# An encoder kernel whose attention iterations have two or three stretches of projection steps instead of four, and whose order is written out up to the first FFN matmuls

## Chip, cores and metric

The kernel runs on one core of a Trainium2 chip. The metric is the device time of one execution in microseconds (us). Before the change: 658.37, the median of 3 runs (658.31 to 658.42).

## What is computed

Two layers of an encoder on 256 tokens of width 1024, float32. Each layer has two attention groups side by side, one output projection, and a gated MLP with a convolution over positions:

```python
for l in range(DEPTH):                                  # 2 layers
    h = rmsnorm(x, attn_norm[l])
    c_q, c_kv, k_r, q_d, k_d, v_d = split(h @ w_in[l])
    o_a = mla_mixer(c_q, c_kv, k_r, ...)                # 8 heads, q and k of 96, v of 64
    q_d, k_d = rmsnorm(q_d heads), rmsnorm(k_d heads)   # per head, over 64
    o_b = dilated_attention(q_d, k_d, v_d, rel_bias)    # 8 heads of 64, with a bias table
    x = x + concat(o_a, o_b) @ w_out[l]
    x = x + conv_ffn(rmsnorm(x, ffn_norm[l]), w_up, conv_w, conv_b, w_down)
```

Both attention groups are a softmax over 256 keys. `conv_ffn` is an up projection to 2 x 2816 columns, a width-3 convolution over positions, `silu(gate) * up`, and the down projection.

## The kernel before

**Split matmuls.** Every large product runs as three f32r matmuls: high x high, low x high, high x low (`mm` triples at L488 to L490, L933 to L936, L1081 to L1083). Weights stream from HBM in units of up to 1024 columns. `Weights` splits each unit: `split_hi` copies it on ACT (L175, tile `wh`), `split_lo` subtracts on DVE (L188, tile `wl`) and, at the last unit of a loaded tile, starts the next load. `fill` does one of each where a buffer is free (6 of each kind); `get` forces what is missing.

**The head iterations.** After the MLA projections, `layer` runs nine iterations, 0 to 8, inside `tc.manual_schedule`: PE, DVE and ACT keep the order in which the code issues; outside it a scheduler orders them. Iteration n handles a pair of heads: `scores` (L549, two S banks), `maxima`, `exponents`, `normalise`; for the pair before it `turn_p` (L589: four transposes of P into a bank, then an ACT copy), `values` (L598, bank O) and `keep_o`; for the pair after it `turn_qk` (L526, bank A) and `keep_qk`. Iterations 0 to 3 have MLA pairs, 4 to 7 dilated ones. MLA heads turn queries and keys one head at a time, so twice an iteration; dilated heads turn a pair at once, scores come out with 64 rows. Between these, `gemm` issues steps from a list: the last key and the value projections of the dilated group (`gk`, `gv`, six matmuls a step, one per token block and unit), then output projection steps (`ou`, three matmuls a step). `COUNTS` gives the number of steps in each iteration, which before are dealt evenly over four stretches. Both P transposes of an iteration use bank A, and so do the query/key turns.

**Background work.** `extras` holds the norm of the dilated queries and keys: `d_begin` copies and squares the projection on ACT, `d_end` sums squares over each head on DVE (L643), `d_factor` computes the reciprocal root on POOL (`rsqrt`, three Newton steps, after two small integer operations on DVE, L279 and L281) and scales the two token blocks there (L290, tile `nat`). The dilated pair of iteration 4 is turned in iteration 3, and reads these tiles.

**From the heads to the FFN.** The last output steps, the residual additions into `X` (`out_end`), the transposes of X for the FFN (`xT_part`: four transposes, multiply by the gain, high half on ACT, low half on DVE, squares for the row norm on ACT) and the first half of the first four up units (`up(0)`, `up(1)` with k 0 to 3) stand outside `manual_schedule`. `ffn_scale` makes the row factor `r2b` out of the squares (three POOL operations, `rsqrt` on DVE, a matmul with ones, an ACT copy). `gate(j)` multiplies by it, convolves, applies silu; `down(j)` follows three units later:

```python
            if j == 0:
                ffn_scale()
            gate(j, pu)
```

Of the kernel before, what the change touches and what calls it, by code (L numbers as in the profile page):

```python
# [10 lines left out]
F32 = mybir.dt.float32  # L11
# [8 lines left out]
P = 128  # L20
# [27 lines left out]
START = 5  # L48
COUNTS = [3, 4, 4, 4, 4, 4, 5, 4, 3]
WARM = 8  # L50
FIRST = 5
# [85 lines left out]
class Weights:  # L137
# [94 lines left out]
def encoder(ctx: ExitStack, tc: tile.TileContext, wpk, x, prm, cst, oh, rb, pos, out):  # L232
# [32 lines left out]
    def tbank():  # L265
        return psa.tile([P, 512], F32, name=nm("A"), tag="A", bufs=1)
# [243 lines left out]
    class Heads:  # L510
# [98 lines left out]
    def layer(l, sx, late, bias):  # L609
# [49 lines left out]

        def d_factor(i, dst):  # L660
            rsqrt(fd[:, i, :], dv[i], 16, neg=i == 0, pool=True)
            for t in range(2):
                d_scale(i, dst, t)

        def d_scale(i, dst, t):
            v3 = dst[:, t, :].rearrange("p (h d) -> p h d", h=HEADS)
            ptt(v3, v3, head_scale(v3, fd[:, i, :], t), ALU.mult)

# [245 lines left out]
        run(gk[:START - 3])  # L914
        hm = Heads(l, True, qm, km, vbox[0], pairs, fq)
        hm.turn_qk(0)
        hm.keep_qk(0)
# [8 lines left out]
        def out_mm(k, t, c, final=False):  # L926
            hi, lo = W.get(u_out[k])
            if not accs:
                accs.extend([[acc(), acc()], [acc(), acc()]])
            p = pairs[k]  # L930
# [25 lines left out]
        def d_end(i, t):  # L956
            d_sum(i, t, sq.pop((i, t)))
            if t:
                d_var(i)

        extras = {
            0: [idle, idle, lambda: d_begin(0, qd, 0, a_q[0]), lambda: d_begin(0, qd, 1, a_q[1])],
            1: [lambda: d_end(0, 0), lambda: (d_end(0, 1), d_factor(0, qd)), lambda: d_begin(1, kd, 0, a_k[0]),
                lambda: d_begin(1, kd, 1, a_k[1])],
            2: [lambda: d_end(1, 0), lambda: (d_end(1, 1), d_factor(1, kd))],
        }
# [4 lines left out]
        def iteration(n):  # L971
# [5 lines left out]
            turns = list(nxt[0].turns(nxt[1])) if nxt else []  # L977
            slots = 4 if nxt or cur else 2
            share = [len(todo) // slots + (i < len(todo) % slots) for i in range(slots)]

# [10 lines left out]

            side = list(extras.get(n, []))

            def background():
                if side:
                    side.pop(0)()

            if n == 3:
                v_evac(0)
                v_evac(1)  # L1000
            if cur:
                cur[0].scores(cur[1])
                cur[0].maxima(cur[1])
            if prev:
                prev[0].turn_p(prev[1])
            if cur:
                cur[0].maxima(cur[1] + 1)
                cur[0].exponents(cur[1])
            W.fill()
            gemm()  # L1010
            if prev:
                prev[0].turn_p(prev[1] + 1)
            if cur:
                cur[0].exponents(cur[1] + 1)
            background()
            gemm()
            if prev:
                prev[0].values(prev[1])
                prev[0].keep_o(prev[1])
            background()  # L1020
            turn_next()
            if cur:
                cur[0].normalise(cur[1])
            W.fill()
            background()
            gemm()
            turn_next()
            if cur:
                cur[0].normalise(cur[1] + 1)
            background()  # L1030
            gemm()
            W.fill()
            while side:
                background()
# [5 lines left out]
        run(steps)  # L1040
        run(ou[5][2:3])
        W.fill()

        def out_end(t, c):
            out_mm(7, t, c, final=True)
            xs = X[:, t, 512 * c:512 * c + 512]
            tt(xs, accs[t][c], xs, ALU.add)

        run(ou[5][3:])
        out_end(0, 0)  # L1050
        out_end(1, 0)
        run(ou[6][2:])
        xT_part(sf, gf, 0, 0)
        xT_part(sf, gf, 1, 0)
        out_end(0, 1)
        out_end(1, 1)
        W.done(u_out[7])
        W.fill()

# [75 lines left out]
        first = [[acc(), acc()], [bank(), bank()]]  # L1135
        for j in range(2):
            up(j, first[j], range(4))
            W.fill()
        xT_part(sf, gf, 0, 1, tbank())
        xT_part(sf, gf, 1, 1, obank())  # L1140
        for j in range(NF):
# [9 lines left out]
            if j == 0:  # L1151
                box["a"] = [[acc(), acc()], [acc(), acc()]]
# [103 lines left out]
```

## Time and profile before

| what | value |
|---|---|
| median of 3 runs | 658.37 us |
| the profiled execution's own time | 658.61 us |
| its span, first to last instruction | 656.8 us |
| mean granted TensorE clock | 0.995 |
| PE busy | 637.5 us, 97% |
| DVE, ACT, POOL busy | 493.9 (75%), 398.2 (61%), 67.5 us (10%) |
| layer 0's heads, 61.2 to 140.5 | PE busy 75.90 of 79.30 us |
| layer 1's heads, 380.3 to 459.5 | PE busy 75.87 of 79.20 us |
| dense FFN part of layer 0, 160.5 to 330 | PE busy 169.5 of 169.5, DVE 134.4 |

The page gives one profiled execution. Busy times are sums of instruction durations, merged where they overlap; matmuls are pipelined, so that a stretch in which PE is called busy can still hold matmuls that start later than they could. The timeline view lists instructions with their start, duration and the idle time before them, with what released it. The name before `<-` is the tile written, the names after it the tiles read.

### The profile page before, as it was taken

Reading aid. Unit: us, or ns where it says so; the run is one execution under the profiler, and the core shown is the slowest. Engines: PE = TensorE matmul, PEld = TensorE weight load, DVE = VectorE, ACT = ScalarE, POOL = GpSimd, SP = SyncE. Lnnn points to the kernel's source line nnn. Section 1 sums busy time; section 2 is a strip of 40 time slices with the busy share of each in tenths; the row PEclk is TensorE's granted clock in tenths of the full one; section 3 lists DMA queues with packets and bytes.
Section 4 is the critical chain, followed back from the end, with each engine's and each line's share of the span. In section 5 each row is a group of like instructions: output and inputs, shape, how many; then the busy total and the mean of one; then the engine's idle time right before and its main releaser. Section 6 shows DMA issues by size and latency. Waiting matters only on the chain.

```text
span 656.8 us, 10655 instructions
## 1 busy us (share of the span) xinstructions
PE 637.5 (97%) x4018; PEld 555.9 (85%) x4018; DVE 493.9 (75%) x1006; ACT 398.2 (61%) x721; POOL 67.5 (10%) x177
## 2 busy tenths in 40 slices
PE   8999899989999999999999989999899999999997
PEld 7967676679999999999899876667899999999996
DVE  4796766778987777778699766667699777777773
ACT  5982966756655555555478467766386555555551
POOL 3950170000000000000001105400000000000000
PEclk8999999999999999999999999999899999999999
DMA  8759431152664555554347423313157545555401
GB/s 305 268 192 181 172 128 65 65 193 84 235 202 185 193 193 193 193 178 158 107 138 277 155 80 113 128 65 129 65 172 277 184 172 176 185 189 189 161 1 64
DMA packets 17707, 105.19 MB, mean 160 GB/s; under 512 B 2102, under 2 KB 3799, under 8 KB 6648
## 3 DMA queue, kind: packets, MB, share of 16 engines
q1 hardware_dynamic: 17368, 104.17, 46.1%
q8 instruction: 31, 0.51, 0.3%
q10 hardware_dynamic: 288, 0.34, 0.2%
q14 instruction: 20, 0.16, 0.1%
HBM read 103.20 MB, written 1.31 MB: 159 GB/s over the span
## 4 chain that ended last, share of the span: by engine, by line
PE 85%; DVE 5%; POOL 4%; ACT 3%; issue 1%; DMA 1%; SPq 0%; DVEq 0%; ACTq 0%; POOLq 0%
PE S L1083 12%; PE S L1082 12%; PE S L1081 12%; PE acc L1127 6%; PE acc L1126 6%; PE acc L1125 6%; PE acc L490 4%; PE acc L489 4%; PE acc L488 4%; PE O L598 3%; PE S L549 2%; PE A L589 2%; PE acc L933 2%; PE acc L936 2%; PE acc L935 2%; POOL s L295 2%
## 5 line engine op out<-in xcount | busy, mean ns | idle before, releaser
L175 ACT ACTIVATE wh<-raw 128x1024 fp32r<-128x1024 f32 (+3 forms) x188 | 193.1, 1035 | 108.7 <-PE S L1082 64.9
L188 DVE TENSOR_TENSOR wl<-raw,wh 128x1024 fp32r<-128x1024 f32 (+3 forms) x188 | 223.2, 1190 | 26.9 <-ACT wh L175 26.1
L1082 PE MATMUL S<-xl,wh 128*128 128x256 f32 x640 | 181.3, 284 | 0.0
L1083 PE MATMUL S<-xh,wl 128*128 128x256 f32 x640 | 180.9, 283 | 0.0
L1081 PE MATMUL S<-xh,wh 128*128 128x256 f32 x640 | 180.3, 283 | 0.0
L1082 PEld LDWEIGHTS S<-xl,wh 128*128 128x128 f32 x640 | 122.7, 192 | 1.5
L1081 PEld LDWEIGHTS S<-xh,wh 128*128 128x128 f32 x640 | 122.4, 192 | 1.5
L1083 PEld LDWEIGHTS S<-xh,wl 128*128 128x128 f32 x640 | 122.7, 192 | 0.1
L284 DVE SCALAR_TENSOR_TENSOR t<-t,prm_s,t 128x255 f32<-128x255 f32 x176 | 73.9, 478 | 1.0 <-ACT t L287 0.9
L1127 PE MATMUL acc<-wl,mh 128*128 128x512 f32 x176 | 69.4, 394 | 0.0
L1125 PE MATMUL acc<-wh,mh 128*128 128x512 f32 x176 | 69.3, 394 | 0.0
L1126 PE MATMUL acc<-wh,ml 128*128 128x512 f32 x176 | 69.2, 393 | 0.0
L488 PE MATMUL acc<-wh,xh 128*128 128x512 f32 (+2 forms) x160 | 61.8, 387 | 1.0 <-ACT nat L287 0.8
L490 PE MATMUL acc<-wl,xh 128*128 128x512 f32 (+2 forms) x160 | 58.5, 366 | 0.3 <-DVE wl L188 0.3
L489 PE MATMUL acc<-wh,xl 128*128 128x512 f32 (+2 forms) x160 | 58.4, 365 | 0.2 <-DVE xl L284 0.2
L287 ACT ACTIVATE t<-A 128x512 f32<-128x512 f32 (+2 forms) x56 | 28.1, 501 | 45.4 <-PE A L526 23.3
L287 ACT ACTIVATE t<-t,prm_s 128x256 f32<-128x256 f32 x88 | 47.6, 589 | 4.7 <-DVE t L275 4.7
L287 ACT ACTIVATE mh<-t 128x256 fp32r<-128x256 f32 x44 | 18.2, 414 | 47.8 <-DVE t L275 47.8
L275 DVE TENSOR_TENSOR t<-S,r2b 128x512 f32<-128x512 f32 (+1 forms) x42 | 27.9, 665 | 24.0 <-PE S L1083 24.0
L1127 PEld LDWEIGHTS acc<-wl,mh 128*128 128x128 f32 x176 | 33.1, 188 | 7.5
L1125 PEld LDWEIGHTS acc<-wh,mh 128*128 128x128 f32 x176 | 33.4, 190 | 5.9
L1126 PEld LDWEIGHTS acc<-wh,ml 128*128 128x128 f32 x176 | 33.1, 188 | 6.1
(168 smaller groups left out, 974.4 us busy)
## 6 DMA issues: line engine op xcount, KB each, us to landing
raw<-in_wpk_dram SPq DMA_DIRECT2D x86, 1024.0 KB, 4.8
raw<-in_wpk_dram SPq DMA_DIRECT2D x3, 896.0 KB, 4.5
raw<-in_wpk_dram SPq DMA_DIRECT2D x3, 768.0 KB, 4.5
raw<-in_wpk_dram SPq DMA_DIRECT2D x2, 816.0 KB, 5.3
Bn<-scr SPq DMA_DIRECT2D x8, 192.0 KB, 11.2
raw<-in_wpk_dram SPq DMA_DIRECT2D x2, 720.0 KB, 5.8
X<-in_x_dram SPq DMA_DIRECT2D x3, 256.0 KB, 5.1
raw<-in_wpk_dram SPq DMA_DIRECT2D x2, 384.0 KB, 5.5
```

Of the source, the lines that this page charges most:

```text
L175: self.nc.scalar.activation(hi[:, :n], self.raw[t][:, o:o + n], AF.Copy, scale=1.0 if g is None else g)
L188: self.nc.vector.tensor_tensor(out=lo[:, :n], in0=raw, in1=hi, op=ALU.subtract)
L287: nc.scalar.activation(o, a, f, **kw)
L488: mm(o, lhs.hi[:, k, sl], rh, start=k == 0, stop=False)
L489: mm(o, lhs.lo[:, k, sl], rh, start=False, stop=False)
L490: mm(o, lhs.hi[:, k, sl], rl, start=False, stop=k == ktot - 1)
L1081: mm(o, hi[:, kp], sf.hi[:, k, :], start=k == 0, stop=False)
L1082: mm(o, hi[:, kp], sf.lo[:, k, :], start=False, stop=False)
L1083: mm(o, lo[:, kp], sf.hi[:, k, :], start=False, stop=k == 7)
L1125: mm(o, m.hi[:, 0, sl], hi[:, cs], start=j == 0, stop=False)
L1126: mm(o, m.lo[:, 0, sl], hi[:, cs], start=False, stop=False)
L1127: mm(o, m.hi[:, 0, sl], lo[:, cs], start=False, stop=j == NF - 1)
```

## The change

It changes the order of work at the heads and after them; the arithmetic stays.

- In an iteration both P transposes follow the scores directly, the second one of a pair in bank O instead of A. The steps come in two or three stretches (`SHARES`): one, one, one in iteration 0; two, one, one where two query/key turns follow; two and two (or three) where one does.
- `turn_next` comes behind the first stretch; `exponents` of the second head and `normalise` of the first behind it; `values` after that. `fill` is taken apart into `fill_hi` and `fill_lo`, which stand at places of their own.
- The exp table is loaded early by an activation of a constant (`act(small(2)[:, :1], ones[:, :1], AF.Exp)`).
- Sums of squares of the dilated heads go to the start of iterations 1 and 2. The scaling of the dilated keys goes from POOL to DVE, at the start of iteration 3; that of the queries stays on POOL.
- `v_evac` goes behind the first exponents of iteration 3, and the output accumulators are dealt out so that the first two steps use the older pair.
- The order is fixed from iteration 8 through the last output steps and the first halves of `up(0)` and `up(1)`. The squares come behind all four transposes. `ffn_scale` and `gate(0)` move from j = 0 to j = 1.

The diff, cut to its core (`ptt` is a POOL operation, `tt` a DVE one):

```diff
+SHARES = {2: (1, 1, 1), 3: (2, 1, 1), 4: (2, 2, 0), 5: (2, 3, 0)}
...
+    def fill_hi(self):
+        if self.n_hi < min(len(self.units), self.n_done + W_BUFS - W_SLACK):
+            self.split_hi()
+
+    def fill_lo(self):
+        if self.n_lo < self.n_hi:
+            self.split_lo()
...
-            pt = tbank()
+            pt = (obank if i % 2 else tbank)()
...
         extras = {
...
+            0: ([], [], [lambda: d_begin(0, qd, 0, a_q[0]), lambda: d_begin(0, qd, 1, a_q[1])]),
+            1: ([lambda: d_end(0, 0), lambda: d_end(0, 1)], [lambda: d_factor(0, qd)],
+                [lambda: d_begin(1, kd, 0, a_k[0]), lambda: d_begin(1, kd, 1, a_k[1])]),
+            2: ([lambda: d_end(1, 0), lambda: d_end(1, 1)], [lambda: d_factor(1, kd, ())], []),
+            3: ([lambda: d_scale(1, kd, 0, tt), lambda: d_scale(1, kd, 1, tt)], [], []),
...
+            kind = 2 if not prev else 3 if len(turns) == 2 else len(todo)
+            share = list(SHARES[kind]) if kind in SHARES and len(todo) == sum(SHARES[kind]) else [2, len(todo) - 2, 0]
...
+            early, middle, late_ = extras.get(n, ([], [], []))
+            if cur:
+                cur[0].scores(cur[1])
+                cur[0].maxima(cur[1])
+                cur[0].maxima(cur[1] + 1)
+            if prev:
+                prev[0].turn_p(prev[1])
+                prev[0].turn_p(prev[1] + 1)
+            run(early)
+            if not early:
+                W.fill_lo()
+            if cur:
+                cur[0].exponents(cur[1])
             if n == 3:
                 v_evac(0)
                 v_evac(1)
...
             gemm()
+            turn_next()
             if cur:
                 cur[0].exponents(cur[1] + 1)
...
+                cur[0].normalise(cur[1])
+            if early:
+                W.fill_lo()
             if prev:
                 prev[0].values(prev[1])
                 prev[0].keep_o(prev[1])
...
+            run(middle)
+            W.fill_hi()
             gemm()
             turn_next()
             if cur:
                 cur[0].normalise(cur[1] + 1)
...
+            run(late_)
+            W.fill_lo()
+            W.fill_hi()
             gemm()
...
+            out_end(0, 0)
+            out_end(1, 0)
+            run(ou[6][2:3])
+            pv0 = gained(0, 0, xT_turn(0, 0))
+            run(ou[6][3:])
+            pv1 = gained(1, 0, xT_turn(1, 0))
+            W.fill_hi()
+            low(0, 0, pv0)
+            low(1, 0, pv1)
+            W.fill_lo()
+            out_end(0, 1)
+            out_end(1, 1)
...
+            up(0, first[0], range(4))
+            W.fill_hi()
+            W.fill_lo()
+            pv2 = gained(0, 1, xT_turn(0, 1, tbank()))
+            up(1, first[1], range(4))
+            pv3 = gained(1, 1, xT_turn(1, 1, obank()))
+            low(0, 1, pv2)
+            low(1, 1, pv3)
+            xT_square(sf, 0, 1)
+            xT_square(sf, 1, 1)
...
             if j == 0:
+                continue
+            if j == 1:
                 ffn_scale()
+                gate(0, first[0])
             gate(j, pu)
```

`gained` is the gain multiplication on DVE and the copy of the high half on ACT, `low` the subtraction of the low half on DVE; together they are what `xT_keep` did.

What stands where, before and after. First PE in iteration 4 of layer 0, from the first P transposes on (A and O are the banks, `acc` the output accumulators, `nat_171` and `nat_172` the dilated queries and keys, `nat_676` the MLA values). Before:

```order
L589 MATMUL A_1389<-cst_s,t_291_1300 128x128 x4
L933 MATMUL acc_1321<-wh_1105,mh_1200 128x512
L935 MATMUL acc_1321<-wh_1105,ml_1201 128x512
L936 MATMUL acc_1321<-wl_1144,mh_1200 128x512
L589 MATMUL A_1406<-cst_s,t_297_1313 128x128 x4
L933 MATMUL acc_1323<-wh_1105,mh_1200 128x512
L935 MATMUL acc_1323<-wh_1105,ml_1201 128x512
L936 MATMUL acc_1323<-wl_1144,mh_1200 128x512
L598 MATMUL O_1418<-t_321_1394,nat_676 64x256
L598 MATMUL O_1418<-t_326_1411,nat_676 64x256
```

and in the change (its line numbers are higher by 9 to 11):

```order
L598 MATMUL A_1390<-cst_s,t_292_1288 128x128 x4
L598 MATMUL O_1397<-cst_s,t_296_1294 128x128 x4
L944 MATMUL acc_1320<-wh_1251,mh_1214 128x512
L946 MATMUL acc_1320<-wh_1251,ml_1215 128x512
L947 MATMUL acc_1320<-wl_1272,mh_1214 128x512
L944 MATMUL acc_1321<-wh_1251,mh_1214 128x512
L946 MATMUL acc_1321<-wh_1251,ml_1215 128x512
L947 MATMUL acc_1321<-wl_1272,mh_1214 128x512
L535 MATMUL A_1416<-cst_s,nat_171 128x128 x2
L535 MATMUL A_1416<-cst_s,nat_172 128x128 x2
L607 MATMUL O_1431<-t_325_1395,nat_676 64x256
L607 MATMUL O_1431<-t_327_1402,nat_676 64x256
```

The second P transposes stand behind the first, in bank O; two output steps follow in one stretch, then the turn of the next pair, and only then the values.

Second, DVE from the last split but one of iteration 2 into iteration 3 (`wl` a weight split, `ml` the low half of an output pair, `nat_172` the dilated keys). Before:

```order
L188 TENSOR_TENSOR wl_1259<-raw_825,wh_1142 128x1024
L279 TENSOR_SCALAR t_286_1274<-A_1269,gqk 96x256
L580 RECIPROCAL s_1278<-s_1167 128x2
L279 TENSOR_SCALAR t_254_1165<-t_254_1165,s_1278 128x256 x2
L188 TENSOR_TENSOR wl_1290<-raw_923,wh_1257 128x1024
L558 TENSOR_REDUCE s_1303<-S_1294 128x2
L284 SCALAR_TENSOR_TENSOR s_1301<-s_1303,fq_189 128x2
L558 TENSOR_REDUCE s_1316<-S_1295 128x2
L284 SCALAR_TENSOR_TENSOR s_1314<-s_1316,fq_189 128x2
L275 TENSOR_TENSOR ml_1346<-O_1340,mh_1345 128x256
L279 TENSOR_SCALAR t_311_1354<-A_1349,gqk 128x256
```

and in the change:

```order
L284 TENSOR_TENSOR ml_1215<-O_1209,mh_1214 128x256
L288 TENSOR_SCALAR s_1218<-s_1172 128x16
L290 TENSOR_SCALAR s_1219<-s_1218 128x16
L288 TENSOR_SCALAR t_287_1264<-A_1259,gqk 96x256
L589 RECIPROCAL s_1268<-s_1152 128x2
L288 TENSOR_SCALAR t_253_1150<-t_253_1150,s_1268 128x256 x2
L189 TENSOR_TENSOR wl_1272<-raw_825,wh_1251 128x1024
L567 TENSOR_REDUCE s_1291<-S_1282 128x2
L293 SCALAR_TENSOR_TENSOR s_1289<-s_1291,fq_189 128x2
L567 TENSOR_REDUCE s_1297<-S_1283 128x2
L293 SCALAR_TENSOR_TENSOR s_1295<-s_1297,fq_189 128x2
L284 TENSOR_TENSOR nat_172<-nat_172,fd_174 128x512 x2
```

The two integer operations that start the keys' reciprocal root (`s_1218`, `s_1219`) now stand behind `ml` and the sums, which were done earlier; the scaling of the keys, two POOL rows before, is a DVE row behind the maxima of iteration 3.

Third, ACT in layer 0's FFN start, up to the row factor (`xh` the high half of the transposed X, `X` rows are the squares, `wh` weight splits). Before:

```order
L287 ACTIVATE t_412_1839,s_896<-X 128x512
L287 ACTIVATE xh_894<-t_411_1835 128x4x128
L287 ACTIVATE t_415_1850,s_896<-X 128x512
L287 ACTIVATE xh_894<-t_414_1846 128x4x128
L175 ACTIVATE wh_1922<-raw_1530 128x1024
L175 ACTIVATE wh_1972<-raw_1678 128x1024
L287 ACTIVATE r2b_1767<-O_1904 128x256
```

and in the change:

```order
L296 ACTIVATE xh_896<-t_412_1819 128x4x128
L296 ACTIVATE xh_896<-t_414_1851 128x4x128
L296 ACTIVATE t_415_1856,s_898<-X 128x512
L296 ACTIVATE t_416_1858,s_898<-X 128x512
L176 ACTIVATE wh_1951<-raw_1488 128x1024
L176 ACTIVATE wh_1962<-raw_1645 128x1024
L176 ACTIVATE wh_1968<-raw_1645 128x1024
L176 ACTIVATE wh_2053<-raw_1726 128x1024
L296 ACTIVATE r2b_1783<-O_1937 128x256
```

The squares of the second half come behind its high halves, and four splits instead of two stand between them and `r2b`.

## Rows read from the trace of the kernel before

**Rows 1.** The page, part 1: busy time, share of the span and instructions of each engine.
```profile
PE 637.5 (97%) x4018; PEld 555.9 (85%) x4018; DVE 493.9 (75%) x1006; ACT 398.2 (61%) x721; POOL 67.5 (10%) x177
```

**Rows 2.** Windows: length; PE, PEld, DVE, ACT, POOL busy us (instructions); PEclk, DMA share, GB/s.
```profile
61.20:140.50 79.30, 75.90 (x403) 53.56 (x401) 54.75 (x142) 55.81 (x129) 16.20 (x39) 1.00 0.38 124
...
140.50:160.50 20.00, 17.93 (x145) 17.51 (x145) 15.13 (x36) 11.24 (x19) 0.81 (x3) 1.00 0.29 106
459.50:479.50 20.00, 17.93 (x132) 17.44 (x132) 13.56 (x32) 9.69 (x18) 0.81 (x3) 0.91 0.26 91
```

**Rows 3.** Who PE waited for: us in total, times, longest us.
```profile
PE A L526 <- DVE t L279: 4.9, 6, 1.0
```

**Rows 4.** PE timeline, iterations 0 to 3: start us, us, instructions, [idle before, releaser].
```profile
61.22 1.89 PE L549 MATMUL S<-t,t 96*128 96x256 f32 x8
...
68.65 0.42 PE L526 MATMUL A<-cst_s,qm 128*96 128x128 f32 x2 [0.98 <-DVE t L279]
...
81.93 1.89 PE L549 MATMUL S<-t,t 96*128 96x256 f32 x8
83.66 0.60 PE L589 MATMUL A<-cst_s,t 128*128 128x128 f32 x4
...
87.41 1.08 PE L598 MATMUL O<-t,nat 128*64 128x256 f32 x8
```

**Rows 5.** PE timeline, a switch from f32 transposes to f32r matmuls.
```profile
71.86 0.60 PE L589 MATMUL A<-cst_s,t 128*128 128x128 f32 x4
72.22 0.48 PE L488 MATMUL acc<-wh,xh 128*128 128x512 f32 x1
72.53 0.39 PE L489 MATMUL acc<-wh,xl 128*128 128x512 f32 x1
72.76 0.40 PE L490 MATMUL acc<-wl,xh 128*128 128x512 f32 x1
```

**Rows 6.** PE timeline, iterations 3 to 8.
```profile
97.43 1.55 PE L598 MATMUL O<-t,nat 128*64 128x256 f32 x8
...
101.26 1.13 PE L549 MATMUL S<-t,t 64*128 64x256 f32 x8
102.32 0.66 PE L589 MATMUL A<-cst_s,t 128*128 128x128 f32 x4
...
130.23 0.60 PE L589 MATMUL A<-cst_s,t 128*128 128x128 f32 x4
```

**Rows 7.** POOL timeline, rsqrt of the dilated keys.
```profile
90.86 0.21 POOL L290 TENSOR_TENSOR s<-s 128x16 f32<-128x16 f32 x1 [0.50 <-DVE s L281]
...
91.78 1.29 POOL L295 TENSOR_SCALAR s<-s 128x16 f32<-128x16 f32 x1
...
97.19 0.22 POOL L290 TENSOR_TENSOR fd<-s,s 128x16 f32<-128x16 f32 x1
```

**Rows 8.** DVE timeline, same stretch, a split of weights.
```profile
91.79 1.22 DVE L188 TENSOR_TENSOR wl<-raw,wh 128x1024 fp32r<-128x1024 f32 x1
```

**Rows 9.** DVE groups by form, 40 to 60 us: count, busy us, mean ns, idle before.
```profile
L275 DVE TENSOR_TENSOR km<-km,fk 128x512 f32<-128x512 f32 x2 | 1.4, 688 | 0.0
```

**Rows 10.** ACT timeline, before the first key evacuation of layer 0.
```profile
40.61 0.47 ACT L287 ACTIVATE km<-acc,rkv 128x256 f32<-128x256 f32 x1 [1.11 <-DVE rkv L284]
```

**Rows 11.** PE timeline, from the last output step to the FFN, layer 0.
```profile
140.20 0.39 PE L936 MATMUL acc<-wl,mh 128*128 128x512 f32 x1
...
143.91 0.36 PE L1082 MATMUL acc<-xl,wh 128*128 128x256 f32 x1
```

**Rows 12.** ACT timeline, the FFN's row factors.
```profile
155.49 0.36 ACT L287 ACTIVATE r2b<-O 128x256 f32<-128x256 f32 x1
```

**Rows 13.** DVE timeline, low half of the first gate's product.
```profile
164.55 0.42 DVE L275 TENSOR_TENSOR ml<-t,mh 128x256 fp32r<-128x256 f32 x1
```

**Rows 14.** PE timeline, first down matmul.
```profile
167.46 0.39 PE L1125 MATMUL acc<-wh,mh 128*128 128x512 f32 x1
```

**Rows 15.** Window of one microsecond in layer 1's FFN start, with the granted clock.
```profile
463.00:464.00 1.00, 1.00 (x7) 0.50 0.76 320
```

More of the change, by code (lines that the diff above doesn't have):

```diff
@@ L658, in d_var, with d_factor, d_scale @@
                     pts(vv, ssd[:, i, t, :], 1.0 / HD, ALU.mult, sx.e1[:, t:t + 1], ALU.add)
-        def d_factor(i, dst):
+        def d_factor(i, dst, toks=range(2)):
             rsqrt(fd[:, i, :], dv[i], 16, neg=i == 0, pool=True)
-            for t in range(2):
-                d_scale(i, dst, t)
-        def d_scale(i, dst, t):
+            for t in toks:
+                d_scale(i, dst, t, ptt)
+        def d_scale(i, dst, t, mul):
             v3 = dst[:, t, :].rearrange("p (h d) -> p h d", h=HEADS)
-            ptt(v3, v3, head_scale(v3, fd[:, i, :], t), ALU.mult)
+            mul(v3, v3, head_scale(v3, fd[:, i, :], t), ALU.mult)
         a_q, a_k, a_v = Accs(), Accs(), Accs()
@@ L915, in layer @@
         hm = Heads(l, True, qm, km, vbox[0], pairs, fq)
+        act(small(2)[:, :1], ones[:, :1], AF.Exp)
         hm.turn_qk(0)
@@ L928, in out_mm @@
             if not accs:
-                accs.extend([[acc(), acc()], [acc(), acc()]])
+                a = [acc() for _ in range(4)]
+                accs.extend([a[0::2], a[1::2]])
             p = pairs[k]
@@ L961, in layer @@
         extras = {
[L962 to L965, printed above, removed]
+            0: ([], [], [lambda: d_begin(0, qd, 0, a_q[0]), lambda: d_begin(0, qd, 1, a_q[1])]),
[3 more added lines that the diff above has]
+            3: ([lambda: d_scale(1, kd, 0, tt), lambda: d_scale(1, kd, 1, tt)], [], []),
         }
@@ L977, in iteration @@
             turns = list(nxt[0].turns(nxt[1])) if nxt else []
-            slots = 4 if nxt or cur else 2
-            share = [len(todo) // slots + (i < len(todo) % slots) for i in range(slots)]
+            kind = 2 if not prev else 3 if len(turns) == 2 else len(todo)
+            share = list(SHARES[kind]) if kind in SHARES and len(todo) == sum(SHARES[kind]) else [2, len(todo) - 2, 0]
             def gemm():
@@ L990, in turn_next @@
                     nxt[0].keep_qk(i)
[L992 to L996, printed above, removed]
+            early, middle, late_ = extras.get(n, ([], [], []))
[11 more added lines that the diff above has]
+                cur[0].exponents(cur[1])
             if n == 3:
@@ L1019, in iteration @@
                 prev[0].keep_o(prev[1])
[L1020 to L1025, printed above, removed]
+            run(middle)
+            W.fill_hi()
             gemm()
@@ L1029, in iteration @@
                 cur[0].normalise(cur[1] + 1)
-            background()
+            run(late_)
+            W.fill_lo()
+            W.fill_hi()
             gemm()
-            W.fill()
-            while side:
-                background()
             assert not todo
@@ L1039, in layer, with out_end, gained, low @@
                 iteration(n)
[L1040 to L1058, printed above, removed]
+            run(steps)
+            run(ou[5][2:])
+            W.fill_hi()
+            W.fill_lo()
+            def out_end(t, c):
+                out_mm(7, t, c, final=True)
+                xs = X[:, t, 512 * c:512 * c + 512]
+                tt(xs, accs[t][c], xs, ALU.add)
+            def gained(t, c, pt):
+                tv = wide()
+                pv = tv.rearrange("p (k t) -> p k t", k=4)
+                tt(pv, pt.rearrange("p (k t) -> p k t", k=4),
+                   gf[:, 4 * c:4 * c + 4].unsqueeze(2).to_broadcast([P, 4, P]), ALU.mult)
+                act(sf.hi[:, 4 * c:4 * c + 4, t * P:t * P + P], pv, AF.Copy)
+                return pv
+            def low(t, c, pv):
+                sl = slice(t * P, t * P + P)
+                tt(sf.lo[:, 4 * c:4 * c + 4, sl], pv, sf.hi.bitcast(F32)[:, 4 * c:4 * c + 4, sl], ALU.subtract)
+            out_end(0, 0)
[10 more added lines that the diff above has]
+            out_end(1, 1)
+            W.done(u_out[7])
+            xT_square(sf, 0, 0)
+            W.fill_hi()
+            W.fill_lo()
+            xT_square(sf, 1, 0)
         r2b = work.tile([P, SEQ], F32, name=nm("r2b"), tag="r2b", bufs=1)
@@ L1135, in layer @@
         first = [[acc(), acc()], [bank(), bank()]]
[L1136 to L1140, printed above, removed]
+        with tc.manual_schedule(engines={mybir.EngineType.PE, mybir.EngineType.DVE, mybir.EngineType.Activation}):
+            up(0, first[0], range(4))
+            W.fill_hi()
+            W.fill_lo()
+            pv2 = gained(0, 1, xT_turn(0, 1, tbank()))
[5 more added lines that the diff above has]
+            xT_square(sf, 1, 1)
         for j in range(NF):
@@ L1148, in layer @@
             if j == 0:
+                continue
+            if j == 1:
                 ffn_scale()
+                gate(0, first[0])
             gate(j, pu)
-            if j == 0:
+            if j == 1:
                 box["a"] = [[acc(), acc()], [acc(), acc()]]
```

13 lines of the change are left out of this document (removed).

## Prediction

> **What bounds the kernel now.** I read the page's busy shares first: PE is busy 637.5 of 656.8 us, 97% [rows 1], so everything this change can win lies in some 19 us of visible PE idle time, plus idle time that hides inside matmul durations. The windows come next. In layer 0's head iterations PE is busy 75.90 of 79.30 us while DVE (54.75) and ACT (55.81) are each under three quarters full [rows 2]: no other engine is the bound there, PE loses time to the order of small dependent steps. The FFN start shows 17.93 of 20.00 in both layers, and in layer 1 also a mean clock of 0.91 [rows 2]. The list of waits names the largest one: PE's query/key transposes waited six times, 4.9 us in all, for DVE [rows 3]. Layer 1's iterations repeat layer 0's, so I work out one layer and double it.
>
> **Prices, from the timeline.** I count PE work from start to next start, because durations overlap. MLA scores take 1.73 us (81.93 to 83.66) and values 1.08 [rows 4]; four transposes 0.36, a 512-column matmul 0.23 (72.53 to 72.76) and the first one after transposes 0.31, so a change of kind costs 0.08; I charge that in both directions [rows 5]. A projection step of six matmuls is then 1.38, an output step of three 0.69. Dilated scores take 1.06 (101.26 to 102.32) [rows 6].
>
> **Iterations 0 to 3, one layer.** They run from 61.22 to 101.26, 40.04 us [rows 4, 6]. Their work: 4 scores 6.92, 6 P transposes 2.16, 3 values 3.24, 11 projection steps 15.18, 4 output steps 2.76, 7 query/key turns 2.52, 22 changes of kind 1.76; together 34.54. So 5.5 us are lost, with examples in the rows: a turn that idled 0.98 [rows 4], values that took 1.55 instead of 1.08 because the second copy of P had just been asked for [rows 6]. The change removes the causes: a turn is now followed by a projection step or by values before the next turn needs bank A, and the second P lies in bank O directly behind the first, with two steps behind both to hide two copies. I do not credit all 5.5.
>
> A wait stays, and grows. The dilated keys may be turned in iteration 3 only when their rsqrt on POOL and their scaling are done. Before, that rsqrt runs from 90.86 to 97.41, 6.55 us [rows 7]. Two of its operations (the row at 91.78 is one) take 1.29 instead of 0.21 us; that one starts within 0.01 us of a weight split of 1.22 us on DVE [rows 7, 8]. The order of the change puts one split into the chain, so I take 6.55 - 1.08 = 5.47. It began 2.37 us after the values of iteration 2 ended (88.49); in the change the key squares are summed earlier (a gain) and a split lies ahead of the low half of the output (a loss of up to 1.22), so I keep about 2.5. Iteration 2 now lasts 1.73 + 0.72 + 5.52 + 1.08 + 0.72 + 8 x 0.08 = 10.4 us, its values end at 6.8, the chain runs from 9.3 to 14.8, that is to 4.4 in iteration 3. Then DVE, which waits there with all behind it, scales twice at 0.69 (the nearest row is the same operation on the MLA keys, [rows 9]): 5.8. PE comes to that turn at 4.0 (scores, both P, two output steps). It waits 1.8 us; bounds are 0 (chain early) and 4 (a second split in it, and everything a microsecond late). I keep back 0.5 more for waits too small to place. Gain: 5.5 - 1.8 - 0.5 = 3.2.
>
> [...]
>
> **Iterations 4 to 7.** From 101.26 to 130.23 are 28.97 us, of which 0.46 belong to two hoisted matmuls [rows 6]. Work: scores 4.24, P 2.88, values 4.32, 17 output steps 11.73, 3 turns 1.08, 16 changes 1.28: 25.53. Lost are 3.0, nearly all as values waiting for the second P copy. Two output steps of 0.69 now stand behind both transposes, against two copies on ACT, so I credit 2.5; 0.5 again for small waits, the first P of iteration 4 after DVE's late start among them. Gain: 2.5.
>
> Edits I cost at nothing: the early table load, since ACT waits for DVE there anyway (1.11 us idle before the next key evacuation, and a split that stood ahead of it is moved behind [rows 10]), though in layer 0 it may push the keys by a few tenths; the permuted accumulators and later v evacuation, which keep the first two output steps off the value accumulators; the weight loads on SP, each issued behind a tile's last split and so moved with it, since the DMA engines are busy 0.38 of this stretch and four loaded tiles wait [rows 2]; the two POOL scales that go to DVE, counted above.
>
> **FFN start.** The last output step starts at 140.20 and lasts 0.23; PE is dense again at 143.91 [rows 11]. In these 3.48 us it does four matmuls of 256 columns (half of 0.23 each) and eight transposes, 1.2 in all, so 2.3 are lost. In the change the first half's transposes stand two to six matmuls earlier, so the high half is there when up(0) starts; the low half of token block 1 comes after it on DVE, 0.6 us late. Against that, the squares and so the row factor now come last: the ACT order puts four weight splits ahead of r2b, each of which needs a buffer that PE frees only as it finishes the first four up units. I expect r2b some 3.6 us later against PE than at 155.49, where it stood 11.6 us ahead of the first down matmul at 167.46 [rows 12, 14]. From its end to the end of the low half of gate 0's product were 9.1 us (155.85 to 164.97, [rows 12, 13]), so that margin is just used up; I charge 0.6 for the mm of ones and the first down. Lost in the change 1.2, gain 1.1 per layer; bounds -2 and +1.9.
>
> **Clock.** In layer 1 the time lost here is followed by a stretch at half clock, 0.50 in the window at 463 [rows 15]; a mean of 0.91 over 20 us costs 1.8 us, and layer 0, with the same PE busy time of 17.93, shows 1.00 [rows 2]. With the loss cut to parts of 0.6 us I expect it to stay away: 1.6; bounds 0 and 1.8.
>
> **Sum.** 2 x (3.2 + 2.5) + 2 x 1.1 + 1.6 = 15.2. The profiled execution took 658.61 us (span 656.8 and 1.8 around it): 643.4. The median of the runs, 658.37, is 0.24 lower: 643.2.
>
> **Rivals.**
> - *The POOL chain does not bind*, and the half microseconds kept back are not lost: 2 x (1.8 + 1.0) = 5.6 less, 637.6. For it: DVE and ACT are far from full. Against it: even before, the rsqrt ended only at 97.41 with two POOL scales to come, as iteration 3 reached its values (97.43, [rows 6, 7]). 0.12.
> - *The new 1.8 us wait drops the clock*, as one of the two FFN starts did before [rows 2, 15]. One or two falls of 1.8 us: 645 to 646.8. For it: layer 1. Against: the wait in iteration 3 is shorter and has dense matmuls on both sides. 0.17. [...]
> - *The gates come too late*: if each of the four splits ahead of r2b, and DVE's four behind them, ends later than I schedule, PE waits at the first down and at the score banks for up to 3 us a layer: 649. 0.10.
> - *Gains lost again inside the FFN*, because DVE starts its dense part behind and never catches up: 657 to 659. 0.03.
> - *Slower*: the key chain. If DVE, which now runs more two-operand work in iteration 2, held each of the other 15 POOL operations of the chain for a split's 1.08 us, the turn of iteration 3 would wait 16 us longer in each layer: 676. It decides against the change from seven held operations on (7 x 1.08 x 2 = 15.1). Against: only one split stands there. 0.03.
>
> **How the numbers follow.** The forecast, with 0.55, is 643.2, its own range 641 to 647. The range to 8 in 10 takes in the clock case, the late gates and the better part of the first rival: 639 to 650. A measurement of this kernel tells 0.2%, 1.3 us, from no change. Faster by more: forecast and the first three rivals, 0.94; within: 0.03; slower: 0.03.
>
> **What would show it.** Values in iterations 4 to 7 at 1.08, not 1.55; no PE wait for DVE at the query/key transposes of iterations 0 to 2; one PE wait of 1 to 3 us in iteration 3 of each layer, for DVE's scaled keys behind POOL; iterations 0 to 8 some 5.7 us shorter per layer; the FFN start's 2.3 us down to 1.2, layer 1's at clock 1.00; r2b about 3 to 4 us later against the first up matmul, with a PE wait under 1 us. It is wrong if the head iterations shorten by less than 4 us a layer, or if the FFN start loses as much as before.

## The result and the profile after

The changed kernel took 642.16 us (median; 642.15 to 643.89) against 658.39 us of the kernel before on the same chip: ratio 0.9756, 95% interval 0.9736 to 0.9775. The profiled execution took 642.16 us, its span 640.4 us, where before they were 658.61 and 656.8. The forecast was 643.2 us, range 639 to 650: 16.2 us came off where 15.2 were expected. The one execution of 643.89 us has a mean clock of 1.000 on record, so a fall of the clock is not what made it longer; what did stays open.

The page, part 1, of the changed kernel, beside [rows 1]:

```profile
PE 627.8 (98%) x4018; PEld 554.6 (87%) x4018; DVE 497.4 (78%) x1010; ACT 395.8 (62%) x723; POOL 58.9 (9%) x173
```

PE has the same 4018 instructions and is busy 9.7 us less: part of the lost time had stood inside long matmul rows, such as values of 1.55 us in [rows 6], and some of it in the stretch of layer 1 at half clock, 0.50 [rows 15]. Windows of the changed kernel, with the columns of [rows 2]: layer 0 from the first scores to the last output step, then 20 us of the FFN start in layer 0 and in layer 1.

```profile
60.80:133.91 73.11, 71.77 (x403) 53.91 (x401) 55.48 (x144) 50.77 (x124) 12.01 (x37) 1.00 0.41 135
133.91:153.91 20.00, 19.58 (x156) 18.88 (x156) 16.79 (x34) 13.87 (x24) 0.58 (x3) 1.00 0.40 137
445.55:465.55 20.00, 19.58 (x156) 18.89 (x156) 16.79 (x34) 13.95 (x24) 0.58 (x3) 1.00 0.37 139
```

The same 403 PE instructions need 73.11 us instead of 79.30. At the FFN start PE is busy 19.58 of 20 us instead of 17.93, and layer 1's clock there is 1.00 instead of 0.91. Who PE waited for, with the columns of [rows 3] (line 535 is line 526 of the kernel before, the query/key turns):

```profile
PE A L535 <- DVE nat L284: 2.7, 4, 1.1
```

The six waits of [rows 3] are gone. What is left at the turns of the iterations is four waits for `nat`, the dilated keys that DVE scales: the wait that the prediction kept. They are two in each layer. Here is its place, PE's timeline from the turn of iteration 3 into iteration 5 (iteration 4 starts at 96.98):

```profile
92.07 0.38 PE L535 MATMUL A<-cst_s,nat 128*128 128x128 f32 x2
93.52 0.33 PE L535 MATMUL A<-cst_s,nat 128*128 128x128 f32 x1 [1.07 <-DVE nat L284]
94.12 0.33 PE L535 MATMUL A<-cst_s,nat 128*128 128x128 f32 x1 [0.27 <-DVE nat L284]
94.38 1.08 PE L607 MATMUL O<-t,nat 128*64 128x256 f32 x8
...
96.98 1.14 PE L558 MATMUL S<-t,t 64*128 64x256 f32 x8
...
104.58 0.66 PE L598 MATMUL A<-cst_s,t 128*128 128x128 f32 x4
105.07 0.60 PE L598 MATMUL O<-cst_s,t 128*128 128x128 f32 x4
...
106.91 0.60 PE L535 MATMUL A<-cst_s,nat 128*128 128x128 f32 x4
107.44 1.08 PE L607 MATMUL O<-t,natb 128*64 128x256 f32 x8
```

From 92.07 to the values at 94.38 are 2.31 us; the turn of iteration 5 needs 0.53 us (106.91 to 107.44), so 1.78 us are lost. The two transposes of P now stand 0.49 us apart (104.58 and 105.07), the second in bank O, and the values of iteration 5 take 1.08 us. Behind the wait stands POOL's chain, with the weight split on DVE that begins inside it:

```profile
87.28 0.21 POOL L299 TENSOR_TENSOR s<-s 128x16 f32<-128x16 f32 x1 [1.78 <-DVE s L290]
...
88.48 1.27 POOL L299 TENSOR_TENSOR s<-s,s 128x16 f32<-128x16 f32 x1
...
92.51 0.22 POOL L299 TENSOR_TENSOR fd<-s,s 128x16 f32<-128x16 f32 x1
```

```profile
88.46 1.21 DVE L189 TENSOR_TENSOR wl<-raw,wh 128x1024 fp32r<-128x1024 f32 x1
...
92.77 1.29 DVE L284 TENSOR_TENSOR nat<-nat,fd 128x512 f32<-128x512 f32 x2 [1.51 <-POOL fd L299]
```

The chain takes 5.45 us (87.28 to 92.73) and has one long row, 1.27 us. At the FFN start PE waited 2.05 us for the high half of the transposed X in the kernel before:

```profile
142.65 0.51 PE L1081 MATMUL acc<-xh,wh 128*128 128x256 f32 x2 [2.05 <-ACT xh L287]
```

In the changed kernel its timeline shows two small losses, one either side of the first up matmul (lines 1106 and 1107), and none at the matmul of ones (149.18) or the first down matmul (159.56):

```profile
133.68 0.40 PE L947 MATMUL acc<-wl,mh 128*128 128x512 f32 x1
134.13 0.39 PE L1106 MATMUL acc<-xh,wh 128*128 128x256 f32 x1
134.86 0.38 PE L1107 MATMUL acc<-xl,wh 128*128 128x256 f32 x1 [0.34 <-DVE xl L284]
...
149.18 0.59 PE L1093 MATMUL O<-t,ones 128*128 128x256 f32 x2
...
159.56 0.39 PE L1150 MATMUL acc<-wh,mh 128*128 128x512 f32 x1
```

Where the 16.4 us of span came from: iterations 0 to 3 went from 40.04 to 36.16 us (60.82 to 96.98), 3.88 a layer; iterations 4 to 7 from 28.51 (28.97 less the 0.46 of two hoisted matmuls) to 26.31, 2.20 a layer; together 12.2 (layer 0 doubled). From the end of the last output step to the first down matmul, layer 0 went from 27.03 to 25.65 us (1.38) and layer 1 from 28.59 to 25.64 (2.95). That is 16.5. The head iterations also begin 0.40 us earlier ([rows 4]: 61.22; now 60.82), and from the last matmul (652.48 before, 635.59 after) to the end of the span it takes 0.5 us longer; I put neither down to the change. Between the first down matmul and the next layer's first scores nothing moved: 212.83 us before, 212.85 after.

### The profile page after: what moved, and what is told of

Read it like the earlier page. It is cut to its first block, busy times and chain, and to the rows that moved or that the text cites. A ratio compares the mean times of both kernels' runs of the same rounds, so it can differ in the third digit from the quotient of the medians.

```text
span 640.4 us, 10656 instructions
## 1 busy us (share of the span) xinstructions
PE 627.8 (98%) x4018; PEld 554.6 (87%) x4018; DVE 497.4 (78%) x1010; ACT 395.8 (62%) x723; POOL 58.9 (9%) x173
## 4 chain that ended last, share of the span: by engine, by line
PE 89%; DVE 5%; POOL 3%; issue 1%; ACT 1%; DMA 1%; SPq 0%; DVEq 0%
PE S L1108 12%; PE S L1107 12%; PE S L1106 12%; PE acc L1152 6%; PE acc L1151 6%; PE acc L1150 6%; PE acc L499 4%; PE acc L497 4%; PE acc L498 4%; PE S L558 3%; PE acc L944 2%; PE O L607 2%; PE acc L947 2%; PE acc L946 2%; PE A L535 1%; POOL s L304 1%
## 5 line engine op out<-in xcount | busy, mean ns | idle before, releaser
L296 ACT ACTIVATE t<-A 96x256 f32<-96x256 f32 (+2 forms) x40 | 18.8, 469 | 43.8 <-PE A L535 26.6
```

What stands on the lines that cost most here:

```text
L296: nc.scalar.activation(o, a, f, **kw)
```

## The experiments

Where a sentence compares with "the change", the 642.16 us above are meant; the kernel before took 658.62, 659.34 and 658.39 us beside the three groups of runs, each on a chip of its own, so a difference of less than 1 us from the change is not told by the medians; where one matters, it is read from the profiles. A ratio is always to the kernel before.

### Is it the order or the bank?

```diff
-            pt = (obank if i % 2 else tbank)()
+            pt = tbank()
```

> The change with the second P back in bank A, all else as it is. Theory (order and bank O belong together): with both P transposes back to back, the second must wait in every iteration until ACT has copied the first out of bank A (a copy of 0.60 us and the way there and back, some 0.9 us; 16 iterations of two layers), so about 14 us slower than the change: 652 to 658 us, and a PE wait for ACT at the P transposes in each iteration. Rival (the order alone brings the gain, the bank is a detail): 642 to 644 us.

Measured: 655.06 us, ratio 0.9946 (0.9934 to 0.9959), 12.9 us slower than the change. The theory holds: sixteen waits, one in each iteration that turns P. PE's waits and the first place in the timeline:

```profile
PE A L598 <- ACT t L296: 11.1, 16, 0.8
```

```profile
69.56 0.60 PE L598 MATMUL A<-cst_s,t 128*128 128x128 f32 x4
70.91 0.66 PE L598 MATMUL A<-cst_s,t 128*128 128x128 f32 x4 [0.76 <-ACT t L296]
```

The other half alone, in the kernel before:

```diff
-            pt = tbank()
+            pt = (obank if i % 2 else tbank)()
```

> The kernel before with one edit: the second P goes to bank O, its place and order stay. Theory (what PE waited for at the values is the second copy of P, asked for only one step earlier, and not the bank): within 1 us of before, 657.5 to 658.5 us, values in iterations 4 to 7 still 1.5 us and more. Rival (bank A was the bottleneck): most of the 12 us of the head iterations come back, 646 to 650 us.

Measured: 657.53 us, ratio 0.9983 (0.9972 to 0.9994), 1.1 us faster than before. From the first scores to those of iteration 7 are 61.82 us (60.80 to 122.62), before 61.78: nothing. Against the expectation, the values do not take 1.5 us and more: the long row has turned into a wait that the timeline can show, and values of 1.08:

```profile
103.09 0.60 PE L589 MATMUL O<-cst_s,t 128*128 128x128 f32 x4
...
105.10 1.08 PE L598 MATMUL O<-t,nat 128*64 128x256 f32 x8 [0.71 <-ACT t L287]
```

From the first scores to the end of the last output step layer 0 takes 79.21 us in the kernel before, 78.76 with the bank alone, 79.44 with the change less the bank, 73.09 with the change. So the bank alone brings 0.45 us a layer, all behind the first scores of iteration 7, the order alone nothing, and the gain belongs to the pair. Which part of the order removed the six waits of [rows 3] was not tested apart: with the bank alone they are all there, with the order alone they are gone and the waits for P stand in their place.

### How many steps must stand behind the transposes?

```diff
-SHARES = {2: (1, 1, 1), 3: (2, 1, 1), 4: (2, 2, 0), 5: (2, 3, 0)}
+SHARES = {2: (1, 1, 1), 3: (2, 1, 1), 4: (0, 4, 0), 5: (0, 5, 0)}
```

> The change with no output step between the P transposes and the next turn or the values in iterations 3 to 7 (shares 0, 4, 0 for 2, 2, 0): the two steps stand behind the values. Theory (two copies of P on ACT take 1.10 us and must be covered by steps behind both transposes): in iteration 4 the copies end 1.79 us after the first P transposes begin, and without steps PE reaches the values about 0.5 us too early, in iteration 7, which has no turn, about 0.9 us: 0.5 x 3 + 0.9 = 2.4 us per layer, 646 to 647.5 us, PE waiting for ACT at the values. Rival (the turn and the bank are cover enough, or the steps moved behind the values hide another wait): 641.5 to 643 us.

> The change with one output step there in place of two (shares 1, 3, 0). Theory (the copies end 1.79 us after the first P transposes begin; in the change the values of iteration 4 start 1.07 us after that, and one step less takes 0.77 of it): nothing but in iteration 7, which has no turn, 0.2 us per layer: 642 to 642.8 us. Rival (what counts is the number of steps, since ACT's copies are held up by other work when they come): 643.5 to 645 us.

(One step: shares 1, 3, 0 and 1, 4, 0.) Measured: no step 652.49 us, ratio 0.9904 (0.9885 to 0.9922); one step 646.95 us, ratio 0.9816 (0.9799 to 0.9833). Both are outside either range. Without steps, iterations 4 to 6 are 0.45, 0.44 and 0.46 us longer and iteration 7 waits 0.74 us at its values, in size what the theory has. The place in iterations 4 to 6 is another: PE waits at the turn, which needs bank A free of the first P, and not at the values:

```profile
102.47 0.66 PE L535 MATMUL A<-cst_s,nat 128*128 128x128 f32 x4 [0.25 <-ACT t L296]
```

With one step, iterations 4 to 6 last 6.53, 6.52 and 7.23 us, what they last in the change (6.53, 6.55, 7.23). What I had overlooked is that the shares serve iteration 3 too, where the step covers POOL's chain; without steps iteration 3 lasts 11.86 us. With one step, iteration 3 of layer 0 lasts 11.07 us instead of 8.91: first a longer wait, then values of nearly double length. Timeline, then two windows:

```profile
94.64 0.33 PE L535 MATMUL A<-cst_s,nat 128*128 128x128 f32 x1 [1.75 <-DVE nat L284]
...
95.65 1.98 PE L607 MATMUL O<-t,nat 128*64 128x256 f32 x8
```

```profile
96.00:98.00 2.00, 2.00 (x9) 0.92 (x6) 1.79 (x5) 1.56 (x7) 0.00 (x0) 0.50 0.04 8
...
410.00:412.00 2.00, 2.00 (x9) 0.97 (x6) 1.90 (x5) 1.56 (x7) 0.00 (x0) 0.50 0.00 0
```

0.67 us are the missing step, 1.5 us (2.16 less 0.67) the clock, which fell to 0.50 in both layers. To separate the two, one step in iterations 4 to 7 only:

```diff
+            SH = {**SHARES, **({4: (1, 3, 0), 5: (1, 4, 0)} if 4 <= n <= 7 else {})}
-            share = list(SHARES[kind])
+            share = list(SH[kind])
```

> The change with one output step between the P transposes and the turn in iterations 4 to 7 only; iteration 3 keeps its two. Theory (in the run with one step everywhere, iterations 4 to 6 began 6.53, 6.52 and 7.23 us after one another as in the change; its loss is iteration 3's, 0.67 us more wait for the keys and then half clock): 641.9 to 642.8 us, and no stretch at half clock in either layer. Rival (the second step is needed in iterations 4 to 7 too): 643.5 to 645 us.

Measured: 642.56 us, ratio 0.9760 (0.9745 to 0.9775); iterations 3 to 6 of layer 0 last 8.91, 6.53, 6.53 and 7.23 us, clock 1.00. From the first scores to the end of the last output step are 73.24 us, in the change 73.09. So one step is cover enough for two copies of P, to within 0.15 us a layer; the second step earns its place in iteration 3.

### The wait for the keys, longer and shorter

```diff
-            3: ([lambda: d_scale(1, kd, 0, tt), lambda: d_scale(1, kd, 1, tt)], [], []),
+            3: ([lambda: d_scale(1, kd, 0, ptt), lambda: d_scale(1, kd, 1, ptt)], [], []),
```

> The change with the two scalings of the dilated keys in iteration 3 back on POOL (1.03 us each by the row of the queries, against 0.65 on DVE). The wait before the second half of the key turn grows by 0.8 us, to about 2.6 us in all. Theory (a wait of 2 us and more there is followed by half clock, as in both layers of the run with one step everywhere, and that costs 1.5 us each): 2 x (0.8 + 1.5) = 4.6 us slower than the change, 645.5 to 647.5 us, with windows at 0.50 behind iteration 3's turn in most cases. Rival (the fall does not hang on the length of the wait): 643.4 to 644.4 us, clock 1.00 there.

Measured: 646.37 us, ratio 0.9814 (0.9801 to 0.9827). Iteration 3 of layer 0 lasts 11.19 us, 2.28 more than in the change. Timeline and windows:

```profile
93.97 0.33 PE L535 MATMUL A<-cst_s,nat 128*128 128x128 f32 x1 [1.47 <-POOL nat L299]
94.97 0.47 PE L535 MATMUL A<-cst_s,nat 128*128 128x128 f32 x1 [0.67 <-POOL nat L299]
```

```profile
96.00:98.00 2.00, 2.00 (x10) 0.96 (x7) 1.96 (x5) 1.56 (x6) 0.00 (x0) 0.50 0.00 0
...
410.00:412.00 2.00, 2.00 (x10) 0.96 (x7) 1.97 (x5) 1.56 (x6) 0.00 (x0) 0.50 0.00 0
```

The two waits are 0.80 us longer together (2.14 for 1.34), and the other 1.48 us of the 2.28 are the lower clock. Moving the two scalings from POOL to DVE, which I had counted as part of the chain, is thus worth 4.2 us, most of it (twice 1.48) kept clock. Now the wait made shorter:

```diff
-            1: (..., [lambda: d_factor(0, qd)],
+            1: (..., [lambda: d_factor(0, qd, ())],
...
-            2: ([lambda: d_end(1, 0), lambda: d_end(1, 1)], [lambda: d_factor(1, kd, ())], []),
+            2: ([lambda: d_end(1, 0), lambda: d_end(1, 1), lambda: d_scale(0, qd, 0, tt),
+                 lambda: d_scale(0, qd, 1, tt), lambda: d_factor(1, kd, ())], [], []),
```

> The change with the rsqrt of the dilated keys started right behind their square sums in iteration 2 (before: behind the values and a weight split), and the scaling of the dilated queries on DVE in iteration 2, where DVE idles 2.03 us, so that POOL is free for the chain. Theory (in iteration 3 the key transposes wait 1.78 us for the chain, nothing else is late there): the chain ends near 90 instead of 92.73 us, the wait falls to 0 to 0.3 us in each layer, 3 to 3.6 us faster than the change: 638.6 to 639.2 us. Rival (the PE wait is only covered by others: copies on ACT, the scaling on DVE behind the maxima): 640.5 to 642.2 us. Rival 2 (a second and third DVE split or subtraction inside the chain blocks POOL again and eats the gain): 641 to 643 us, with POOL rows of 1.27 us twice or more in the chain.

Measured: 639.87 us, ratio 0.9712 (0.9699 to 0.9726), 2.3 us faster than the change, outside all three ranges. PE, then POOL, then DVE in layer 0:

```profile
91.91 0.53 PE L535 MATMUL A<-cst_s,nat 128*128 128x128 f32 x3
92.70 0.33 PE L535 MATMUL A<-cst_s,nat 128*128 128x128 f32 x1 [0.27 <-DVE nat L284]
92.96 1.08 PE L607 MATMUL O<-t,nat 128*64 128x256 f32 x8
```

```profile
84.59 0.21 POOL L299 TENSOR_TENSOR s<-s 128x16 f32<-128x16 f32 x1 [0.50 <-DVE s L290]
...
85.52 1.29 POOL L304 TENSOR_SCALAR s<-s 128x16 f32<-128x16 f32 x1
86.90 0.22 POOL L299 TENSOR_TENSOR s<-s,s 128x16 f32<-128x16 f32 x1
...
88.23 1.29 POOL L304 TENSOR_SCALAR s<-s 128x16 f32<-128x16 f32 x1
...
91.10 0.22 POOL L299 TENSOR_TENSOR fd<-s,s 128x16 f32<-128x16 f32 x1
```

```profile
85.53 1.22 DVE L189 TENSOR_TENSOR wl<-raw,wh 128x1024 fp32r<-128x1024 f32 x1
86.67 0.42 DVE L284 TENSOR_TENSOR ml<-O,mh 128x256 fp32r<-128x256 f32 x1
...
88.24 1.22 DVE L189 TENSOR_TENSOR wl<-raw,wh 128x1024 fp32r<-128x1024 f32 x1
```

The turn takes 1.05 us instead of 2.31; iteration 3 is 1.24 us shorter, iteration 4 0.18 longer. The chain starts 2.69 us earlier but ends only 1.41 earlier, because two splits now stand in it, and each goes with a POOL row of 1.29 us. The theory's wait was there to be won; what the second rival names took part of the gain, though less than its range has.

### The FFN start and the clock

The old code from the last output steps to the gates, in the changed kernel (its core):

```diff
-            run(ou[5][2:])
-            W.fill_hi()
-            W.fill_lo()
...
+        run(ou[5][2:3])
+        W.fill()
...
+            if j == 0:
+                ffn_scale()
+            gate(j, pu)
```

> The change with the old code from the last steps of the output projection to the gates of the FFN (old order, chosen by the scheduler, gate 0 ahead of the second up unit), head iterations as changed. Theory (1.4 us per layer from the order there, and 1.6 more in layer 1 because PE's clock no longer falls): 645.5 to 647 us, with a stretch at half clock behind the FFN start of layer 1, or of layer 0, where the loss is the same. Rival 1 (the fall of the clock hung on where the kernel stood in time and does not come back): 644.5 to 645.2 us, clock 1.00 in both. Rival 2 (the new order only moves a wait into the FFN): 642 to 643.5 us.

Measured: 646.66 us, ratio 0.9805 (0.9789 to 0.9820). Its five runs took 645.06, 645.16, 646.66, 646.79 and 648.05 us, in steps of about 1.5 us; the profile is of the longest, and shows the lower clock in two places:

```profile
138.00:140.00 2.00, 2.00 (x11) 2.00 (x11) 1.92 (x3) 1.24 (x3) 0.43 (x1) 0.50 0.18 70
...
410.00:412.00 2.00, 2.00 (x7) 1.62 (x6) 1.97 (x5) 2.00 (x6) 0.00 (x0) 0.54 0.00 0
...
454.00:456.00 2.00, 2.00 (x20) 2.00 (x19) 1.90 (x3) 1.25 (x3) 0.43 (x1) 1.00 0.21 86
```

The first is behind the FFN start of layer 0, where in the kernel before the clock had held; layer 1's FFN start, with the same wait of 2.05 us, kept 1.00, where before it fell [rows 15]:

```profile
452.25 0.51 PE L1086 MATMUL acc<-xh,wh 128*128 128x256 f32 x2 [2.05 <-ACT xh L296]
```

The second is iteration 3 of layer 1, behind the same wait of 1.08 and 0.28 us that the change has there without a fall. So the order is worth 1.4 us a layer (645.1 less 642.16 is 2.9; from the end of the last output step to the first down matmul, layer 1 here takes 27.03 us, in the change 25.64), and a fall is a further 1.5 or so that one execution has in one place, another elsewhere or not at all. That the three levels of the five runs are none, one and two falls is my reading; only the longest was profiled, but the mean clocks on record, 1.000 and 1.000, 0.997 and 0.997, 0.992, rank the five runs the same way.

### The early table load, and the two gains together

```diff
-        act(small(2)[:, :1], ones[:, :1], AF.Exp)
```

> The change without its early one-column exponential (which brings ACT's table for Exp in while ACT idles). Theory (the prediction's: ACT waits there anyway, the edit is worth nothing): 641.9 to 642.6 us. Rival (the load of 1.28 us moves ahead of the first exponents of iteration 0; behind them on ACT wait the copies of the keys of iteration 1, so the second half of its scores waits for DVE's scaled queries again, 0.74 us in each layer as in the kernel before, or the whole 1.28): 643.6 to 644.8 us, with a PE wait for DVE at the scores, twice.

Measured: 643.15 us, ratio 0.9760 (0.9745 to 0.9774). Neither range has it, and the medians alone would not tell it from the change; the profile does. Iteration 0 lasts 7.25 us in both layers instead of 6.74 and 6.78, and a turn in it waits for DVE:

```profile
60.89 1.89 PE L558 MATMUL S<-t,t 96*128 96x256 f32 x8
...
66.27 0.42 PE L535 MATMUL A<-cst_s,qm 128*96 128x128 f32 x2 [0.23 <-DVE t L288]
...
68.14 1.89 PE L558 MATMUL S<-t,t 96*128 96x256 f32 x8
```

What fits is a load of 1.28 us on ACT, after the maxima have come and ahead of the exponents. In the kernel before it stood there, in the change it stands at 37.94, 23 us ahead of the scores; the row is of the kernel before:

```profile
63.27 1.28 ACT L287 ACT_TABLE_LOAD   x1 [2.85 <-DVE s L284]
```

The edit that I had costed at nothing is worth 0.5 us a layer. Last, the early keys together with another order in the first half of up unit 0:

```diff
+                if j == 0 and ks[0] == 0 and half == 0:
+                    for k in ks:
+                        kp = slice(k * P, k * P + P)
+                        mm(o, hi[:, kp], sf.hi[:, k, :], start=k == 0, stop=False)
+                        mm(o, lo[:, kp], sf.hi[:, k, :], start=False, stop=False)
+                    for k in ks:
+                        mm(o, hi[:, k * P:k * P + P], sf.lo[:, k, :], start=False, stop=False)
+                    continue
```

> The early start of the keys' rsqrt (as in keys_early) and at the FFN start the first up unit in another order: all products with the high half of the first four blocks first, those with the low half last. Theory (the low half is late by 0.61 us after the first up matmul, and eight matmuls of 0.12 us with the high half cover that): 1.2 us faster than with the early keys alone (639.9 us), 638.5 to 639 us, and no PE wait for DVE's low half. Rival (the wait comes back at the next thing late there, the second half of the transposes or the splits): 639.5 to 640 us.

Measured: 638.66 us, ratio 0.9695 (0.9681 to 0.9710), 3.5 us faster than the change and the fastest of the kernels here. From the end of the last output step to the first down matmul are 25.04 us in both layers, in the change 25.65 and 25.64. The low half is no longer waited for:

```profile
133.02 0.39 PE L1108 MATMUL acc<-xh,wh 128*128 128x256 f32 x1
...
134.07 0.64 PE L1111 MATMUL acc<-xl,wh 128*128 128x256 f32 x4
```

## Why the prediction was right

- **Iterations 0 to 3**, forecast 3.2 us a layer, measured 3.88. The kept wait was sized well: chain 5.45 us (5.47), wait 1.78 us (1.8). What did not appear are the 0.5 us kept back for small waits: iterations 1 and 2 last 10.25 and 10.26 us and show no PE wait. Part of the gain, 0.5 us, is the early table load, which I had put at nothing because ACT idles there; in the kernel before, the load (1.28 us at 63.27) stands behind that idle time, ahead of the exponents and of the key copies queued behind them. So the turn that idled 0.98 us in iteration 0 [rows 4], which I put down to the order alone, was only in part the order's: the order takes that wait from 0.98 to 0.23 us, the early load the rest. The size of the total came out near with that share in the wrong place.
- **Iterations 4 to 7**, forecast 2.5, measured 2.20. Here the size was off: I counted 3.0 us as lost, nearly all at the values, and kept 0.5 back. But the four values rows of the kernel before (1.64, 1.66, 1.17 and 1.65 us) exceed 1.08 by only 1.8 us in all. Iteration 4 now runs without a PE wait and lasts 6.53 us, while my prices give 5.98 of work and four changes of kind of 0.08, 6.30. The price of the changes was too low: from the turn to the values it is 0.53 us for 0.36 of transposes. No PE wait is left in these iterations. "Two steps behind both" was more than needed: one covers the copies.
- **FFN start**, forecast 1.1 a layer, measured 1.38 in layer 0. The low half's 0.6 us came as worked out (134.25, the first up matmul's end, to 134.86). The 0.6 us for the row factor did not: r2b starts 16.15 us after the first up matmul instead of 12.84, 3.3 us later (forecast 3.6), and that is early enough: from its end to the end of the low half of gate 0's product are 8.3 us (150.64 to 158.98), not 9.1, and the first matmul that reads the low half starts at 159.79. Instead 0.2 us go ahead of the first up matmul.
- **Clock**, forecast 1.6, measured 1.57 (2.95 less 1.38). Right in size, but as a property of layer 1 it was too simple: the run with the old FFN start shows the fall in the other layer (0.50 at 138 to 140). That the clock stays up behind the shorter loss is borne out in the change's profile, 1.00 in both layers' windows; for the other runs with the new FFN start it is not shown.
- **Rivals.** "POOL does not bind" is refuted by the wait; started early, the chain still ends 0.3 us after DVE is free for it. "The new wait drops the clock" did not happen in the change's profile, but in one other execution with the same wait, and with longer waits at that turn each time. It was rightly the largest rival. "Slower, by splits that hold POOL" has its price in the rows, 1.05 to 1.08 us a split (1.27 to 1.29 us instead of 0.21 to 0.22); the change puts one split there, not seven. "The gates come too late" and "gains lost again inside the FFN" did not happen: PE does not wait at the first down matmul, and from there to the next layer the time is what it was.
- **The sum.** The parts are off by 0.68, 0.30 (the other way) and 0.28 us a layer, 2.5 us if the signs are left out, the total by 1.0: that it came so near is in part luck.

## What to carry to other kernels

A shared bank and the order of its users are one decision: here either half alone left the heads within half a microsecond a layer of what they took before, and both together gained 12.2 us. Count cover by time, from the request to the last copy (1.79 us here) against PE's own work between, and look for every place that the same table of shares serves. A long chain like POOL's here (5.45 us) should start as soon as its inputs are there, with DVE's weight splits kept out of its stretch (each cost the chain 1.05 to 1.08 us); and a PE wait of one or two microseconds, in this kernel, is to be priced with the half clock that may follow it, about 1.5 us.

## What the runs showed of the hardware

- **Half clock after a wait.** Of the profiles here, four (the change, no early table load, one step in iterations 4 to 7, old FFN start) have iteration 3's wait of some 1.07 and 0.27 us in both layers: in one of these eight places the clock fell, to 0.54 in a window of 2 us, in seven it stayed at 1.00. Three (no step, one step, keys scaled on POOL) have 1.47 to 1.92 and 0.27 to 0.67 us: it fell in all six, to 0.50 or 0.54. Where I worked out the price, a fall cost about 1.5 us (1.49 with one step, 1.48 with the keys on POOL). The length of the wait alone does not decide: the old FFN start's one wait of 2.04 to 2.2 us (the kernel before, the same with bank O, the change with the old FFN start) was followed by a fall in three of the five places whose clock was read, in layer 1 of the first two (0.50) and in layer 0 of the third (0.50). Why it comes in one layer and not in the other behind the same wait is not shown.
- **POOL beside DVE.** In the reciprocal roots' chains, POOL operations that otherwise took some 0.2 us took 1.27 to 1.29 us where a weight split of 1.21 or 1.22 us began on DVE within 0.02 us of them, and two splits in the keys' chain (the kernel before, the early keys) went with two such rows. The 0.42 us subtraction of the low half (86.67) held up nothing: POOL's row at 86.90 took 0.22 us.
